# Two more k tiles by seven products in the gate/up groups of a decoder layer, with adding transfers for two of the sums

## The chip, the cores and the metric

The kernel runs on one core of one Trainium2 chip. The metric is the device time of one execution in microseconds; three executions of the kernel before gave a median of 1983.21 us.

## The reference, cut to what matters

One decoder layer on 256 tokens of width 2048, all in float32: a half-step SwiGLU feed-forward block, a token mixer, and a second half-step block, each followed by a layer norm.

```python
def _swiglu(x, w_gate, w_up, w_down):
    return (jax.nn.silu(x @ w_gate) * (x @ w_up)) @ w_down
...
    h = _layer_norm(ALPHA * h + 0.5 * _swiglu(h, ffn1_w_gate[l], ffn1_w_up[l], ffn1_w_down[l]), ...)
    mix = _mixer(h, ...)
    h = _layer_norm(ALPHA * h + mix, ...)
    h = _layer_norm(ALPHA * h + 0.5 * _swiglu(h, ffn2_w_gate[l], ffn2_w_up[l], ffn2_w_down[l]), ...)
```

`w_gate` and `w_up` are 2048x5632 each. The change is in `x @ w_gate` and `x @ w_up`, in both feed-forward blocks.

## The kernel before

Every float32 product is made of three matmuls on two reduced parts: `split` makes `hi` by a cast on ACT and `lo = src - hi` by a subtraction on DVE, and `triple` adds `xh*wh + xh*wl + xl*wh`. The moving operand is a 128x512 piece of the weights, the stationary one a 128x128 piece of the activations (16 k tiles of 128 rows by 2 blocks of 128 tokens).

The gate and up weights are laid out side by side in chunks of 512 columns, 22 chunks per feed-forward block. The first two chunks are done by `project`. The other 20 are done in ten **groups** of two chunks (`w0`, `w1`) by `Hybrid.group`. There are two such blocks in the layer, so 20 groups. A weight block read from memory is 128x1024 (two k tiles of one chunk, 512 KB) and is called j = 0 to 7.

In a group the k tiles 0 to 7 (blocks j = 0 to 3 of both chunks) are taken by **seven products** in place of eight (a scheme of Strassen's kind on two halves of k by two chunks, and two halves of k by two token blocks). The weights' quarters are "11" (`w0`, j 0 and 1), "12" (`w1`, j 0 and 1), "21" (`w0`, j 2 and 3), "22" (`w1`, j 2 and 3); each is two blocks, halves s = 0 and 1. The products are called forms 1, 5, 6, 7, 2, 4, 3. Form 5 wants 11+12, form 6 wants 11+12+22, form 7 wants 12+22, form 4 wants 11+12+22+21; forms 1, 2 and 3 take 11, 21 and 22 as they are. The sums are made in place in the tiles `sraw` by DVE (line 344). The activations' seven forms are made once per feed-forward block by `Seven`. The k tiles 8 to 15 (blocks j = 4 to 7 of each chunk) are taken plainly.

The work is a row of **units**. A unit of a form's half has 6 matmuls, a plain unit 12. Each unit has a load (SP asks for the block), a preparation (a sum where there is one, and `split` into a pair of `wring` tiles) and its matmuls. In a group the units stand in this order, with "1.0" for form 1 half 0 and "p4" for the plain block j = 4 of `w0` (a prime for `w1`): 1.0 1.1 p4, 5.0 5.1 p5, 6.0 6.1 p6, 7.0 7.1 p7, 2.0 2.1 p4', 4.0 4.1 p5', 3.0 3.1 p6' p7'. That is 14 x 6 + 8 x 12 = 180 matmuls.

What sets the order and holds the units back:

- `look(3, 4)` lets loads run up to three units ahead of their preparation and preparations up to four ahead of their matmuls.
- There are six `wring` pairs in these groups (`set_ring(6)`). The ACT cast of a unit can begin only when PE is done with the unit six before it.
- Plain blocks land in four rotating tiles `raw`, the quarters in `sraw` tiles of their own. A load waits until the last reader of its tile is done, and SP issues loads in order.
- Within these limits a scheduler orders each engine's instructions when the program is built; on the chip each engine runs its list in order.
- The bank sums of a group are finished by `sum_done`: DVE `gus` (128x512, line 728), ACT `sg`, DVE `hb` (128x256, line 719), and after every group two DVE transposes `blocks` and eight POOL transfers `hT` (line 608).
- Activations and most buffers live in 40 slots of 4 KB per partition (`act_tile`).

Of the kernel before, what the change touches and what calls it, by code (L numbers as in the profile page):

```python
# [11 lines left out]
F32 = mybir.dt.float32  # L12
# [47 lines left out]
def layer_kernel(ctx: ExitStack, tc: tile.TileContext, a: dict, out: bass.AP):  # L60
# [188 lines left out]
    class Seven:  # L249


        def __init__(self, raws, order=None, plain=None):

            self.raws, self.order, self.plain = raws, order, plain
            self.at_ = {}
            self.steps = [self.sums, lambda: self.pair(self.fa, 5, 6), lambda: self.pair(self.fb, 7, 3),
                          self.as_is, self.minus]

        def as_is(self):
# [38 lines left out]
    class Hybrid:  # L298


        def __init__(self, x, seven, k_tiles, small=False):

            self.x, self.seven, self.k_tiles = x, seven, k_tiles
            self.raws = {n: [act_tile([P, 1024], F32, "sraw") for _ in range(2)] for n in ("11", "12", "22")}
            self.raws["21"] = self.raws["12"] if small else [act_tile([P, 1024], F32, "sraw") for _ in range(2)]
            self.snaps = [[act_tile([P, 2, 512], F32, "snap") for _ in range(2)] for _ in range(1 if small else 2)]
            self.last = (3, 2, 4) if small else (2, 4, 3)
            self.turn = 0

        def group(self, w0, w1, done):  # L310
            banks = {}
# [3 lines left out]
            R = self.raws  # L315
            blocks = {"11": (w0, 0), "12": (w1, 0), "21": (w0, 2), "22": (w1, 2)}

            plan = {1: ("11", "11", None, "X"), 5: ("12", "11", ("11", "12"), "Z"), 6: ("22", "11", ("11", "22"), "X"),
# [14 lines left out]
            def seventh(p, s):  # L333
# [3 lines left out]
                def load():  # L337
                    w, j0 = blocks[load_block]
                    nc.sync.dma_start(R[load_block][s], w[j0 + s])

                def prep():
                    t = R[src][s]
                    if add is not None:
                        V.tensor_tensor(out=t, in0=t, in1=R[add[1]][s], op=ALU.add)  # L344
                    pair = next_pair()
                    split(*pair, t)
                    st["pair"] = [v.rearrange("p (g n) -> p g n", g=G) for v in pair]

                def now():
# [11 lines left out]
            def plain(n, j, last=False):  # L361
# [24 lines left out]
                unit(load, prep, now)  # L386

            end = self.k_tiles // G - 1
            for p, n, j in zip((1, 5, 6, 7) + self.last, (0, 0, 0, 0, 1, 1, 1), (4, 5, 6, 7, 4, 5, 6)):
                for s in range(2):  # L390
                    seventh(p, s)
                plain(n, j)
            plain(1, end, True)
# [311 lines left out]
    def ffn(n, x, wgu, wdn, residual, g, bt, each, first=None, between=None, nxt=None, cols=None):  # L705
# [40 lines left out]

        seven = Seven(x.raws)

# [15 lines left out]
        look(3, 4)  # L764
        hy = Hybrid(x, seven, KD)
        for p in range(1, KF // 4):
            if p == KF // 4 - 1:
                for i, q in enumerate((3, 4, 0)):
                    later(3 + 3 * i, lambda q=q: get_h(q))
                later(13, lambda: split_h(3))  # L770
                later(16, lambda: split_h(4))
            hy.group(wgu[2 * p], wgu[2 * p + 1],
                     lambda n, b, bank, snap, op, p=p: sum_done(2 * p + n, b, bank, snap, op))
        ln = LayerNorm(0.5, residual, g, bt, each, nxt, cols, ((24, 26, 48, 50), (94, 97, 100, 103)))
# [426 lines left out]

    xq = Acts(KD, "x", (0, 1))

# [117 lines left out]
```

## Time and profile before

| | |
|---|---|
| median of 3 executions | 1983.21 us (1982.7 to 1984.22) |
| the profiled execution | 1983.64 us, of which span 1981.9 us |
| matmuls | 8832 |
| PE, DVE, ACT, POOL busy | 1967.9, 1770.4, 1247.6, 248.8 us |
| groups of the first block | from about 60 to 460 us of the span |
| groups of the second block | from about 1340 to 1740 us of the span |

The span runs from the first to the last instruction; the rest of the execution's time lies around it. Engines are PE (matmuls), PEld (loads of the stationary operand), DVE, ACT, POOL and SP (which issues transfers). A busy time is the union of the durations of an engine's instructions, and on DVE and PE an instruction is issued before the one ahead of it has ended. So the time that one costs in a full queue is the distance from start to start, not its duration.

### The profile page before, as it was taken

How to read it: one execution, taken by the hardware profiler on the slowest of the kernel's cores; microseconds unless marked ns; L12 is line 12 of the kernel's file. 1: busy time of each engine (PE TensorE's matmuls, PEld its weight loads, DVE VectorE, ACT ScalarE, POOL GpSimd, SP SyncE). 2: the span in 40 equal slices, each digit the busy share in tenths (PEclk: the TensorE clock that was granted, in tenths of full speed). 3: DMA queues.
4: the chain of work that ended last, by engine and by line, in shares of the span. 5: the costliest groups of instructions: out<-in, count | busy, mean ns of one | idle time of the engine just before them, and what ended most of it. 6: DMA issues, size and time to landing. Idle time of an engine off the chain costs nothing.

```text
span 1981.9 us, 25344 instructions
## 1 busy us (share of the span) xinstructions
PE 1967.9 (99%) x8832; PEld 1628.9 (82%) x8832; DVE 1770.4 (89%) x2089; ACT 1247.6 (63%) x1571; POOL 248.8 (13%) x463
## 2 busy tenths in 40 slices
PE   9999999999999999999999999999999999999997
PEld 7888888888888888888888888888888888888886
DVE  7999999999799889999877676799999999998986
ACT  6666666666556566666667764566666666665552
POOL 0111101012010011002223130001011100121000
PEclk9999999999999999999999999999999999999999
DMA  8667766658678666677667667657676666596763
GB/s 323 220 212 237 262 211 202 218 199 313 232 228 274 204 221 246 220 245 250 228 215 249 228 225 264 220 208 242 225 257 229 201 216 228 186 327 225 256 222 125
DMA packets 133649, 460.50 MB, mean 232 GB/s; under 512 B 19424, under 2 KB 19472, under 8 KB 133520
## 3 DMA queue, kind: packets, MB, share of 16 engines
q1 hardware_dynamic: 109296, 389.59, 57.4%
q0 software_dynamic: 24224, 69.29, 11.2%
q8 instruction: 69, 1.13, 0.2%
q14 instruction: 60, 0.49, 0.1%
HBM read 429.97 MB, written 28.84 MB: 231 GB/s over the span
## 4 chain that ended last, share of the span: by engine, by line
PE 90%; DVE 4%; DMA 3%; issue 2%; ACT 1%; SPq 0%; POOL 0%; DVEq 0%; ACTq 0%; POOLq 0%
PE mm L203 29%; PE mm L204 29%; PE mm L202 29%; DVE wring L150 2%; DMA raw<-in_dn_dram 1%; PE tr L203 1%; PE tr L204 1%; PE tr L202 1%; ACT wring L149 1%; DVE sraw L344 0%; PE tr L571 0%; DMA hraw<-hT 0%; DMA raw<-in_wgd_dram 0%; DMA raw<-in_gu_dram 0%; DVE sraw L519 0%
## 5 line engine op out<-in xcount | busy, mean ns | idle before, releaser
L149 ACT CAST wring<-raw 128x1024 fp32r<-128x1024 f32 (+2 forms) x499 | 516.2, 1039 | 338.7 <-PE mm L204 236.6
L150 DVE TENSOR_TENSOR wring<-raw,wring 128x1024 fp32r<-128x1024 f32 (+2 forms) x499 | 596.7, 1202 | 117.0 <-ACT wring L149 110.3
L149 ACT CAST wring<-sraw 128x1024 fp32r<-128x1024 f32 x436 | 453.7, 1052 | 217.4 <-PE mm L204 98.1
L150 DVE TENSOR_TENSOR wring<-sraw,wring 128x1024 fp32r<-128x1024 f32 x436 | 523.6, 1217 | 35.2 <-ACT wring L149 31.0
L204 PE MATMUL mm<-wring,h 128*128 128x512 f32 (+2 forms) x1296 | 499.3, 386 | 0.0
L203 PE MATMUL mm<-wring,h 128*128 128x512 f32 (+2 forms) x1296 | 498.5, 385 | 0.3 <-DVE wring L150 0.3
L202 PE MATMUL mm<-wring,h 128*128 128x512 f32 (+2 forms) x1296 | 498.6, 385 | 0.0
L203 PE MATMUL mm<-wring,xs 128*128 128x512 f32 x776 | 302.3, 390 | 0.3 <-DVE wring L150 0.3
L202 PE MATMUL mm<-wring,xs 128*128 128x512 f32 x776 | 302.5, 390 | 0.0
L204 PE MATMUL mm<-wring,xs 128*128 128x512 f32 x776 | 302.1, 389 | 0.0
L204 PEld LDWEIGHTS mm<-wring,h 128*128 128x128 f32 x1296 | 243.5, 188 | 48.9 <-DVE h L150 1.4
L202 PEld LDWEIGHTS mm<-wring,h 128*128 128x128 f32 x1296 | 243.5, 188 | 48.8 <-ACT h L149 1.0
L203 PEld LDWEIGHTS mm<-wring,h 128*128 128x128 f32 x1296 | 243.5, 188 | 48.7 <-DVE wring L150 0.9
L344 DVE TENSOR_TENSOR sraw<-sraw,sraw 128x1024 f32<-128x1024 f32 x208 | 249.9, 1211 | 1.6 <-DMA sraw<-in_gu_dram 1.5
L608 POOL DMA_DIRECT2D hT<-blocks x176 | 95.7, 551 | 766.5 <-DVE blocks L606 711.5
L203 PEld LDWEIGHTS mm<-wring,xs 128*128 128x128 f32 x776 | 145.7, 188 | 31.5 <-DVE wring L150 1.6
L202 PEld LDWEIGHTS mm<-wring,xs 128*128 128x128 f32 x776 | 145.7, 188 | 31.1 <-ACT snap L321 0.7
L204 PEld LDWEIGHTS mm<-wring,xs 128*128 128x128 f32 x776 | 145.7, 188 | 30.1
L203 PE MATMUL mm<-wring,x 128*128 128x512 f32 x384 | 149.6, 390 | 0.6 <-DVE wring L150 0.6
L202 PE MATMUL mm<-wring,x 128*128 128x512 f32 x384 | 149.5, 390 | 0.3 <-ACT wring L149 0.3
L204 PE MATMUL mm<-wring,x 128*128 128x512 f32 x384 | 149.3, 389 | 0.0
L203 PEld LDWEIGHTS mm<-wring,x 128*128 128x128 f32 x384 | 72.1, 188 | 16.2 <-DVE wring L150 1.3
(268 smaller groups left out, 1921.2 us busy)
## 6 DMA issues: line engine op xcount, KB each, us to landing
raw<-in_gu_dram SPq DMA_DIRECT2D x191, 512.0 KB, 4.4
sraw<-in_gu_dram SPq DMA_DIRECT2D x160, 512.0 KB, 5.2
raw<-in_dn_dram SPq DMA_DIRECT2D x140, 512.0 KB, 4.6
sraw<-in_dn_dram SPq DMA_DIRECT2D x36, 512.0 KB, 5.3
hraw<-hT POOLq DMA_DIRECT2D x68, 256.0 KB, 5.7
raw<-in_w_out_dram SPq DMA_DIRECT2D x32, 512.0 KB, 4.4
raw<-in_wgd_dram SPq DMA_DIRECT2D x24, 512.0 KB, 4.6
hT<-blocks POOLq DMA_DIRECT2D x176, 64.0 KB, 2.3
```

What stands on the lines that cost most here:

```text
L149: S.copy(hi, src)
L150: V.tensor_tensor(out=lo, in0=src, in1=hi.bitcast(F32), op=ALU.subtract)
L202: PE.matmul(o, xh, wh, start=first, stop=False, skip_group_check=again)
L203: PE.matmul(o, xh, wl, start=False, stop=False, skip_group_check=again)
L204: PE.matmul(o, xl, wh, start=False, stop=last, skip_group_check=again)
L344: V.tensor_tensor(out=t, in0=t, in1=R[add[1]][s], op=ALU.add)
L608: nc.gpsimd.dma_start(to.rearrange("(g r) (i f) -> i r g f", g=4, i=4)[i], t[32 * i:32 * (i + 1), :].rearrange("r (g f) -> r g f", g=4))
```

## The change

The k tiles 8 and 9 (block j = 4 of both chunks) are taken by seven products as well: the four 128x512 quarters of it are a11, a21 (tile `u0`, from `w0`) and a12, a22 (tile `u1`, from `w1`). Two plain units of 12 matmuls become four units `n1`, `n5`, `n6`, `n7` that hold the forms (1, 2), (5, 4), (6) and (7, 3), with 6, 6, 3 and 6 matmuls. A group has 177 matmuls. Their sums are four DVE additions of 128x512. The two blocks are loaded by `load_nine` while the group before is under way, into tiles `nine` of their own. The units now stand so: 1.0 n1 1.1 p5, 5.0 n5 5.1 p6, 6.0 n6 6.1 p7, 7.0 n7 7.1, 2.0 2.1 p5', 4.0 4.1 p6', 3.0 3.1 p7'.

Of the eight 128x1024 additions on DVE four stay (forms 5 and 6). For form 7 the quarter 22 is added to 12, and for form 4 the quarter 21 to 11, by transfers from memory that add into the `sraw` tile; POOL issues them, four a group. The quarter 21 goes through the four `raw` tiles. The activations' forms of k tiles 8 and 9 are made once per block by `Seven.ninth`, which keeps a third raw quad of the activations; the forms 2 and 4 are taken from the tiles that the plain units use.

```diff
-    def __init__(self, raws, order=None, plain=None):
+    def __init__(self, raws, order=None, plain=None, ninth=False):
...
+            if ninth:
+                self.steps.insert(3, self.ninth)
...
-            self.raws["21"] = self.raws["12"] if small else [act_tile([P, 1024], F32, "sraw") for _ in range(2)]
+            self.small = small
+            if small:
+                self.raws["21"] = self.raws["12"]
+            else:
+                self.nine = [act_tile([P, 2, 512], F32, "nine") for _ in range(3)]
...
+        def load_nine(self, w0, w1):
+            for t, w in zip(self.nine, (w0, w1)):
+                nc.sync.dma_start(t.rearrange("p a n -> p (a n)"), w[4])
...
+            adds = {} if self.small else {5: ("12", "22"), 6: ("11", "21")}
...
-                    nc.sync.dma_start(R[load_block][s], w[j0 + s])
+                    if load_block == "21" and not self.small:
+                        st["raw"] = wpool.tile([P, 1024], F32, tag="raw", name=nm("raw"), bufs=4)
+                    nc.sync.dma_start(st["raw"] if "raw" in st else R[load_block][s], w[j0 + s])
 
                 def prep():
-                    t = R[src][s]
-                    if add is not None:
+                    t = st["raw"] if "raw" in st else R[src][s]
+                    if add is not None and (self.small or p in (5, 6)):
                         V.tensor_tensor(out=t, in0=t, in1=R[add[1]][s], op=ALU.add)
                     pair = next_pair()
                     split(*pair, t)
...
+                    if p in adds:
+                        to, block = adds[p]
+                        w, j0 = blocks[block]
+                        nc.gpsimd.dma_start(R[to][s], w[j0 + s], accum_op=ALU.add)
...
+            def ninth(p):
+                u0, u1, v = self.nine
+                a11, a21, a12, a22 = u0[:, 0], u0[:, 1], u1[:, 0], u1[:, 1]
+                forms = {1: (1, 2), 5: (5, 4), 6: (6,), 7: (7, 3)}[p]
+                names = {1: "XY", 5: "ZW", 6: "X", 7: "XZ"}[p]
...
+                    src = {1: u0, 5: v, 6: u0[:, 0:1], 7: u1}[p]
+                    if p == 5:
+                        for out, in0, in1 in ((v[:, 0], a11, a12), (a11, v[:, 0], a22), (v[:, 1], a11, a21)):
+                            V.tensor_tensor(out=out, in0=in0, in1=in1, op=ALU.add)
+                    elif p == 7:
+                        V.tensor_tensor(out=a12, in0=a12, in1=a22, op=ALU.add)
+                    split(*(t[:, :len(forms)] for t in pair), src)
...
+                for p, n, j in zip((1, 5, 6, 7) + self.last, (0, 0, 0, None, 1, 1, None), (5, 6, 7, None, 5, 6, None)):
+                    seventh(p, 0)
+                    if p in (1, 5, 6, 7):
+                        ninth(p)
+                    seventh(p, 1)
+                    if n is not None:
+                        plain(n, j)
+                    if p == 4 and following is not None:
+                        self.load_nine(*following)
             plain(1, end, True)
...
-        seven = Seven(x.raws)
+        seven = Seven(x.raws, None, x, True)
...
+        hy.load_nine(wgu[2], wgu[3])
...
-    xq = Acts(KD, "x", (0, 1))
+    xq = Acts(KD, "x", (0, 1, 2))
...
-    h2 = Acts(KD, "h2", (0, 1))
+    h2 = Acts(KD, "h2", (0, 1, 2))
```

The prediction speaks of three places in a group. The first is on DVE, behind the preparation of unit 7.1. Before, `sraw_82` and `sraw_83` are quarter 21, `sraw_76` and `sraw_77` quarter 11, and the rows are 2.0, the sum for 4 and its splits:

```order
L150 TENSOR_TENSOR wring_19_119<-sraw_83_457,wring_18_118 128x1024
L344 TENSOR_TENSOR sraw_76_450<-sraw_76_450,sraw_82_456 128x1024
L150 TENSOR_TENSOR wring_17_117<-raw_178_1481,wring_16_116 128x1024
L344 TENSOR_TENSOR sraw_77_451<-sraw_77_451,sraw_83_457 128x1024
L150 TENSOR_TENSOR wring_15_115<-sraw_76_450,wring_14_114 128x1024
L150 TENSOR_TENSOR wring_5_105<-sraw_77_451,wring_4_104 128x1024
```

In the changed program `sraw_77` and `sraw_78` are quarter 11, `sraw_79` and `sraw_80` quarter 12, `nine_83` is `u0`, `nine_84` is `u1`, and `nine_85` is the sums' tile. The same stretch, on DVE:

```order
L150 TENSOR_TENSOR wring_5_105<-sraw_78_457,wring_4_104 128x1024
L150 TENSOR_TENSOR wring_19_119<-nine_84_463,wring_18_118 128x1024
L150 TENSOR_TENSOR wring_17_117<-sraw_80_459,wring_16_116 128x1024
L150 TENSOR_TENSOR wring_15_115<-raw_179_1514,wring_14_114 128x1024
L150 TENSOR_TENSOR wring_5_105<-raw_180_1524,wring_4_104 128x1024
L436 TENSOR_TENSOR nine_85_464<-nine_83_462,nine_84_463 128x512
L150 TENSOR_TENSOR wring_3_103<-raw_181_1532,wring_2_102 128x1024
L438 TENSOR_TENSOR nine_84_463<-nine_84_463 128x512
L150 TENSOR_TENSOR wring_21_121<-sraw_77_456,wring_20_120 128x1024
L150 TENSOR_TENSOR wring_19_119<-sraw_78_457,wring_18_118 128x1024
```

Rows one to five are the splits of 6.1, n7, 7.1, 2.0 and 2.1. The row L436 is the next group's first sum of the ninth block: the scheduler put it three splits behind the last reader (n7) of the tile that the next group's `u1` is loaded into.

The second place is SP's list of loads over the same time. Before, with `sraw_78` quarter 12:

```order
L339 DMA sraw_78_452<-in_gu1_dram 128x1024
L368 DMA raw_184_1565<-in_gu1_dram 128x1024
L339 DMA sraw_79_453<-in_gu1_dram 128x1024
L339 DMA sraw_82_456<-in_gu1_dram 128x1024
L368 DMA raw_188_1605<-in_gu1_dram 128x1024
```

Now:

```order
L404 DMA raw_182_1565<-in_gu1_dram 128x1024
L371 DMA sraw_79_458<-in_gu1_dram 128x1024
L336 DMA nine_84_463<-in_gu1_dram 128x1024
L371 DMA sraw_80_459<-in_gu1_dram 128x1024
L404 DMA raw_183_1594<-in_gu1_dram 128x1024
```

The load of `u1` for the next group stands between the two of quarter 12.

The third place is POOL's list, which before holds only the `hT` transfers in a group:

```order
L608 DMA hT1_122<-blocks_171_1394 32x4x128 x4
L608 DMA hT1_122<-blocks_172_1400 32x4x128 x4
L736 DMA hraw_324_3111<-hT1_122 128x512 x2
L608 DMA hT1_122<-blocks_197_1692 32x4x128 x4
L608 DMA hT1_122<-blocks_198_1698 32x4x128 x4
```

Now a group has its four adding transfers (L383) around them:

```order
L383 DMA sraw_79_458<-in_gu1_dram 128x1024
L681 DMA hT1_122<-blocks_147_1113 32x4x128 x4
L681 DMA hT1_122<-blocks_148_1119 32x4x128 x4
L383 DMA sraw_80_459<-in_gu1_dram 128x1024
L383 DMA sraw_77_456<-in_gu1_dram 128x1024
L383 DMA sraw_78_457<-in_gu1_dram 128x1024
```

The one into `sraw_80` stands behind the eight `hT` transfers; the one into `sraw_78` can start when the split of 6.1 is done.

More of the change, by code (lines that the diff above doesn't have):

```diff
@@ L308, in __init__, with group @@
             self.turn = 0
-        def group(self, w0, w1, done):
+        def load_nine(self, w0, w1):
+            for t, w in zip(self.nine, (w0, w1)):
+                nc.sync.dma_start(t.rearrange("p a n -> p (a n)"), w[4])
+        def group(self, w0, w1, done, following=None):
             banks = {}
@@ L772, in ffn @@
             hy.group(wgu[2 * p], wgu[2 * p + 1],
-                     lambda n, b, bank, snap, op, p=p: sum_done(2 * p + n, b, bank, snap, op))
+                     lambda n, b, bank, snap, op, p=p: sum_done(2 * p + n, b, bank, snap, op),
+                     (wgu[2 * p + 2], wgu[2 * p + 3]) if p < KF // 4 - 1 else None)
         ln = LayerNorm(0.5, residual, g, bt, each, nxt, cols, ((24, 26, 48, 50), (94, 97, 100, 103)))
```

38 lines of the change are left out of this document (33 added, 5 removed).

## The prediction

> **What bounds the kernel now.** I read the page first, for the whole; then the windows of the gate/up groups; then the timeline of DVE, ACT and PE inside one group; and last the loads.
>
> ```profile
> span 1981.9 us, 25344 instructions
> PE 1967.9 (99%) x8832; PEld 1628.9 (82%) x8832; DVE 1770.4 (89%) x2089; ACT 1247.6 (63%) x1571; POOL 248.8 (13%) x463
> ...
> PE 90%; DVE 4%; DMA 3%; issue 2%; ACT 1%; SPq 0%; POOL 0%; DVEq 0%; ACTq 0%; POOLq 0%
> ```
>
> PE is busy all the time and carries 90% of the chain that ended last, so a matmul less should be time less. The windows show how much room the others have where the change is made (after the busy times: granted clock, share of the DMA engines, GB/s):
>
> ```profile
> 140.00:180.00 40.00, 40.00 (x179) 33.10 (x178) 38.75 (x41) 25.58 (x31) 3.53 (x7) 1.00 0.66 219
> 1420.00:1460.00 40.00, 40.00 (x178) 33.14 (x177) 38.75 (x41) 25.58 (x31) 3.54 (x7) 1.00 0.65 220
> 460.00:500.00 40.00, 40.00 (x178) 33.13 (x177) 38.16 (x49) 27.11 (x36) 13.04 (x24) 1.00 0.94 332
> ```
>
> In the groups (first two rows) PE is never idle and DVE is busy 38.75 of 40 us: two engines at their bound, PE just ahead. ACT has room.
>
> **What the groups' instructions cost.** The timeline of two groups, DVE, then ACT, then PE (start, duration):
>
> ```profile
> 207.08 0.42 DVE L719 TENSOR_TENSOR hb<-gus,sg 128x256 f32<-128x256 f32 x1
> 207.42 1.22 DVE L344 TENSOR_TENSOR sraw<-sraw,sraw 128x1024 f32<-128x1024 f32 x1
> 208.56 1.21 DVE L150 TENSOR_TENSOR wring<-sraw,wring 128x1024 fp32r<-128x1024 f32 x1
> 209.69 1.22 DVE L150 TENSOR_TENSOR wring<-raw,wring 128x1024 fp32r<-128x1024 f32 x1
> 214.23 0.68 DVE L728 TENSOR_TENSOR gus<-mm,snap 128x512 f32<-128x512 f32 x1
> 214.83 1.21 DVE L150 TENSOR_TENSOR wring<-sraw,wring 128x1024 fp32r<-128x1024 f32 x1
> 223.03 3.49 DVE L150 TENSOR_TENSOR wring<-sraw,wring 128x1024 fp32r<-128x1024 f32 x3
> 226.43 1.22 DVE L344 TENSOR_TENSOR sraw<-sraw,sraw 128x1024 f32<-128x1024 f32 x1
> ```
>
> ```profile
> 248.00 1.05 ACT L149 CAST wring<-sraw 128x1024 fp32r<-128x1024 f32 x1 [0.71 <-PE mm L204]
> ```
>
> ```profile
> 216.47 0.39 PE L202 MATMUL mm<-wring,xs 128*128 128x512 f32 x1
> 227.35 0.39 PE L202 MATMUL mm<-wring,xs 128*128 128x512 f32 x1
> 257.27 0.39 PE L202 MATMUL mm<-wring,xs 128*128 128x512 f32 x1
> ```
>
> From start to start a DVE instruction costs 1.135 us at 1024 columns (207.42 to 208.56 to 209.69), 0.60 at 512 (214.23 to 214.83) and 0.34 at 256 (207.08 to 207.42). The PE rows are unit 1.1 of one group (216.47), its unit 6.1, 48 matmuls later (227.35), and 1.1 of the next group, 180 matmuls later (257.27): 10.88/48 = 40.80/180 = 0.2267 us each. A group before takes 40.8 us.
>
> **Matmuls.** 3 fewer in each of 20 groups: 60 x 0.2267 = 13.6 us. If PE stayed busy, the time would be 1983.6 - 13.6 = 1970.0, and a group 177 x 0.2267 = 40.1 us.
>
> **DVE's work.** Before, a group has 22 splits and 8 sums of 1024, four `gus` and two transposes of 512, four `hb`: 30 x 1.135 + 6 x 0.60 + 4 x 0.34 = 39.0 us. After: 20 splits and 4 sums of 1024, in the ninth block 3 splits of 1024, one of 512 and four sums of 512, the rest the same: 27 x 1.135 + 11 x 0.60 + 4 x 0.34 = 38.6. So DVE gains 0.4 us and PE 0.7: DVE may stand still 1.5 us in a group where it could 1.8. ACT gets 1.5 casts more, in the 14 us it has free in 40. `Seven.ninth` and the dropped `as_is` split of the feed-forward forms are a few DVE instructions once per block, in the second plain chunk; there DVE prepares 8 units in the time of 96 matmuls (9 of 21.8 us), which hides them, and some 3 us would be their price without it. SP issues 16 loads a group as before, and the `raw` tiles still turn eight times (two plain blocks less, the two of quarter 21 more), so neither costs by itself.
>
> **The lead between DVE and PE.** What counts is whether each split is ready before its matmuls. Before, the split of 1.1 starts 216.47 - 208.56 = 7.9 us ahead of its matmuls. From there to the split of 6.1 (the second of the three from 223.03, at 224.16) DVE needs 15.6 us and PE 10.9, so 3.2 us are left, less the split's own 1.22: PE finds 6.1 ready by 2.0 us. After, the cast of 1.1 waits for PE's end with the unit six before it (the ACT row's wait on PE is this one). That unit is p6', and 36 matmuls lie between it and 1.1 where there were 42. So the lead at 1.1 is at most 36 x 0.2267 - 1.05 (cast) - 0.1 = 7.0 us. From 1.1 to 6.1 DVE now has 12 rows of 1024, 7 of 512 and 2 of 256: 18.5 us; PE has 57 matmuls: 12.9. Left: 7.0 - 5.6 - 1.22 = 0.2 us. PE still just fits. Any DVE wait beyond about 1.4 us a group (1.5, less a little) goes to PE in full.
>
> **The ninth block's load, the term that decides.** DVE's list has the next group's first ninth sum four rows behind the split of n7, which is the last reader of the `nine` tile to be loaded. The load goes out 1.25 us after that split starts; DVE is at the sum after 4 x 1.135 = 4.5 us. So DVE waits L - 3.3 us, L being the load's time to landing; behind it in DVE's list stand the splits of p5', 4.0 and 4.1; ACT's casts for them are not held. The loads of the groups from 100 to 420 us, 64 of line 339, and the medians of like transfers over the whole span, with POOL's at the end:
>
> ```profile
> L339 SPq DMA_DIRECT2D sraw<-in_gu_dram x64: 327/328/444, 104.1 to 405.7; - x64
> ...
> DMA to landing us min/median/max: 3.1/5.0/7.1
> ```
>
> ```profile
> raw<-in_gu_dram SPq DMA_DIRECT2D x191, 512.0 KB, 4.4
> ...
> z<-in_x_dram POOLq DMA_DIRECT2D x4, 512.0 KB, 8.4
> gb<-in_ln_b_dram POOLq DMA_DIRECT2D x6, 512.0 KB, 5.2
> ```
>
> ```profile
> L608 POOL DMA_DIRECT2D hT<-blocks x176 | 95.7, 551 | 766.5 <-DVE blocks L606 711.5
> ```
>
> L is 3.1 to 7.1; the wait 0 to 3.8 us. SP's list puts a load of quarter 12 just ahead and another just behind, and an adding transfer (into `sraw_78`, released by the split before n7's) runs beside it, so I take 5.4, nearest to the median 5.0 and somewhat above: a wait of 2.1. That is 0.7 over the 1.4, so a group takes 40.1 + 0.7 + 0.3 (ACT's `snap` copies and the 0.2 us fit at 6.1, both of which I can place no closer than this) = 41.1 us, 0.3 over before: +6 us over 20 groups.
>
> **The adding transfers.** No row shows one. From below it is a POOL load (5.2 us, the `gb` row), from above twice the slowest kind (16.8, 2 x the `z` row). Into `sraw_79` and `sraw_77` there are 16 and 10 us before the cast that reads them. Into `sraw_80` it must wait for POOL's eight `hT` issues (0.55 us each) and has 8; into `sraw_78`, from the split of 6.1 to the cast of 4.1, DVE's rows leave 6.75 us, and with the 2.1 of the ninth block's wait 8.9. At 8.4, the nearest loaded case, this hides; each us beyond costs 20 us in all. For the transfer engines:
>
> ```profile
> q1 hardware_dynamic: 109296, 389.59, 57.4%
> ```
>
> By this row 0.524 MB cost 1.53 us of all 16 engines, four more a group 6.1: the share goes from 0.66 to about 0.81. The window 460:500 above has 0.94 with PE full, so share alone doesn't stop PE; it lengthens L.
>
> [...]
>
> **The ends of the blocks.** In the last group of each block the split of an `h` tile, which lay elsewhere before, now stands ahead of the split of 6.1, where nothing is to spare:
>
> ```profile
> 236.75 1.29 DVE L150 TENSOR_TENSOR h<-hraw,h 128x512 fp32r<-128x512 f32 x2
> ```
>
> Two of 512 cost 1.2 us, twice: +2.4 us. Bounds: 0 if the lead is larger there, 6 if POOL's `hraw` issues ahead of the adding transfers make these late too.
>
> **Sum.** -13.6 (matmuls) + 20 x 1.0 (0.7 + 0.3 of waits) + 2.4 = +8.8 on the profiled execution's 1983.6 gives 1992.4; that execution lies 0.4 above the median of the three, so against the median 1992.
>
> **Rivals.** *Faster*: the ninth load lands in 4.4 us or less (the median of `raw`). Then DVE waits 1.1, inside the 1.4, and PE is fed but for the 0.3: 20 x (0.7 - 0.3) = 8 us gained, less 2.4, or all 13.6 if those small terms vanish: 1970 to 1978. For it: before, PE never waits in spite of DVE's 97%. It turns at L of about 4.7. Against it: three more transfers beside this load. *No change*: L of 4.8 to 5.1, 1979 to 1987. [...] *The change doesn't do what it says*: excluded for the matmuls, which the lists show 60 fewer.
>
> **How the numbers follow.** Slower by waits as summed 0.38 (1987 to 2010); adding transfers late 0.13 (2010 to 2060); no change 0.17; faster 0.32. About 0.2% (4 us) is what a measurement here can tell from no change. So faster 0.32, same 0.17, slower 0.51, and the time 1992. The range runs from 1969, the whole 13.6 gained, to 2025, which leaves out most of the late transfers; the slower case's own range is 1987 to 2010.
>
> **What would show it.** PE with idle time before unit 5.1 or 6.1, released by DVE's split; DVE idle at the sum of line 436, released by the DMA of `nine`, about 2 us in each group; groups 41 us apart; no wait of ACT on `sraw` beyond a few tenths. Wrong if the sum of line 436 waits under 1.2 us (then faster), or if ACT's casts of `sraw` wait on POOL's transfers (then slower by more).

## The result, and the profile after

The changed kernel takes 2047.18 us (median of 6 executions, 2044.87 to 2052.33) against 1983.20 us (6 executions, 1982.7 to 1984.22): ratio 1.0325, 95% interval 1.0311 to 1.0338. It is 64 us slower, and 55 us slower than predicted. The profiled execution took 2048.91 us. Its page:

```profile
span 2046.8 us, 25513 instructions
...
PE 1984.4 (97%) x8772; PEld 1629.2 (80%) x8772; DVE 1759.0 (86%) x2139; ACT 1269.3 (62%) x1613; POOL 319.9 (16%) x543
...
PE 58%; DVE 25%; DMA 8%; issue 6%; ACT 1%; POOL 0%; SPq 0%; DVEq 0%; ACTq 0%; POOLq 0%
```

The 60 matmuls are gone (8772), yet PE is busy 17 us longer, and it carries only 58% of the chain that ended last; DVE has 25% and transfers 8%. The windows of two stretches in the groups (columns as before: PE, PEld, DVE, ACT, POOL, granted clock, share of the DMA engines, GB/s):

```profile
140.00:180.00 40.00, 37.58 (x158) 30.37 (x157) 35.33 (x37) 26.40 (x30) 7.91 (x12) 0.96 0.85 254
1440.00:1480.00 40.00, 37.53 (x158) 30.42 (x157) 35.34 (x39) 24.33 (x30) 7.93 (x12) 0.96 0.86 249
```

158 matmuls in 40 us where there were 179. Both engines that were full now stand still at times, and the granted clock is 0.96 where it was 1.00. From the first `gus` of a group to the next group's it is 43.9 us on average over the 18 distances inside the blocks (39.8 to 45.6, the shortest at the ends of the blocks), where it was 40.7. Twenty times the difference is 63 us, so nearly all of the loss lies in the groups. The waits (engine, line, what it waited for: us in all, times, longest):

```profile
DVE nine L436 <- DMA nine<-in_gu_dram: 78.8, 18, 6.8
...
PEld mm L203 <- DVE wring L150: 51.3, 32, 2.6
PE mm L203 <- DVE wring L150: 39.9, 29, 2.1
...
ACT wring L149 <- DMA sraw<-in_gu_dram: 31.1, 20, 3.8
```

DVE waits 18 times at the first sum of the ninth block, 4.4 us on average, and PE then waits for DVE's splits. One such wait on DVE, and SP's list before it:

```profile
197.10 1.22 DVE L150 TENSOR_TENSOR wring<-nine,wring 128x1024 fp32r<-128x1024 f32 x1
...
199.37 2.36 DVE L150 TENSOR_TENSOR wring<-raw,wring 128x1024 fp32r<-128x1024 f32 x2
208.55 0.69 DVE L436 TENSOR_TENSOR nine<-nine,nine 128x512 f32<-128x512 f32 x1 [6.82 <-DMA nine<-in_gu_dram]
```

```profile
196.08 0.33 SPq L371 DMA_DIRECT2D sraw<-in_gu_dram  x1
198.35 0.33 SPq L336 DMA_DIRECT2D nine<-in_gu_dram  x1
```

The split of n7 starts at 197.10, SP asks for `u1` at 198.35 (1.25 us later, as foreseen), and the sum starts at 208.55: this load took 10.2 us. What the transfers cost, by the DMA queues (packets, MB, share of the 16 engines' span; the first line is POOL's queue before, the rest is after) and the issues (median us to landing):

```profile
q0 software_dynamic: 24224, 69.29, 11.2%
```

```profile
q0 software_dynamic: 35744, 111.23, 22.3%
...
raw<-in_gu_dram SPq DMA_DIRECT2D x191, 512.0 KB, 5.6
...
sraw<-in_gu_dram POOLq DMA_DIRECT2D x80, 512.0 KB, 7.3
nine<-in_gu_dram SPq DMA_DIRECT2D x40, 512.0 KB, 6.8
```

POOL's queue had 11.2% of 1981.9 us before, 222 us; now 22.3% of 2046.8, 456. The 80 adding transfers so took 2.93 us of all 16 engines each.

**The clock.** The prediction did not have this. Eleven stretches of 3.41 or 6.83 us inside the groups run at half clock, 13 times 3.41 us in all; before, there was none but the one at the very end. One of them, as three windows of 3.41 us, and PE's matmuls through it:

```profile
145.00:148.41 3.41, 1.58 (x6) 1.09 (x7) 3.41 (x4) 2.40 (x3) 1.62 (x3) 0.99 0.90 236
148.41:151.82 3.41, 3.41 (x10) 2.64 (x9) 3.41 (x4) 2.48 (x3) 0.85 (x1) 0.51 1.01 203
151.82:155.23 3.41, 3.41 (x17) 2.80 (x16) 2.75 (x3) 1.81 (x2) 0.85 (x1) 1.00 1.01 217
```

```profile
147.26 0.50 PE L203 MATMUL mm<-wring,xs 128*128 128x512 f32 x1 [1.83 <-DVE wring L150]
147.59 0.39 PE L204 MATMUL mm<-wring,xs 128*128 128x512 f32 x1
...
149.08 0.63 PE L203 MATMUL mm<-wring,x 128*128 128x512 f32 x1
149.50 0.63 PE L204 MATMUL mm<-wring,x 128*128 128x512 f32 x1
149.93 0.63 PE L202 MATMUL mm<-wring,x 128*128 128x512 f32 x1
```

PE waits 1.83 us for DVE's split, is busy only 1.58 of 3.41 us, and in the next 3.41 us its matmuls come 0.427 us apart (149.08, 149.50, 149.93) in place of 0.227. Such a window holds eight matmuls, which cost 1.6 us more. If PE is the bound in all 13 windows, they cost 21 us; that is an estimate.

### The profile page after: what moved, and what is told of

Its sections match the earlier page's. It is cut to its first block, busy times and chain, and to the rows that moved or that the text cites. A ratio compares the mean times of both kernels' runs of the same rounds, so it can differ in the third digit from the quotient of the medians.

```text
span 2046.8 us, 25513 instructions
## 1 busy us (share of the span) xinstructions
PE 1984.4 (97%) x8772; PEld 1629.2 (80%) x8772; DVE 1759.0 (86%) x2139; ACT 1269.3 (62%) x1613; POOL 319.9 (16%) x543
## 3 DMA queue, kind: packets, MB, share of 16 engines
q0 software_dynamic: 35744, 111.23, 22.3%
## 4 chain that ended last, share of the span: by engine, by line
PE 58%; DVE 25%; DMA 8%; issue 6%; ACT 1%; POOL 0%; SPq 0%; DVEq 0%; ACTq 0%; POOLq 0%
PE mm L203 18%; PE mm L204 18%; PE mm L202 18%; DVE wring L150 15%; DMA nine<-in_gu_dram 6%; DVE sraw L376 3%; DVE gus L801 2%; DVE hb L792 1%; DMA sraw<-in_gu_dram 1%; DVE nine L436 1%; DVE blocks L679 1%; ACT wring L149 1%; PE tr L202 1%; PE tr L204 1%; PE tr L203 1%
## 5 line engine op out<-in xcount | busy, mean ns | idle before, releaser
L149 ACT CAST wring<-sraw 128x1024 fp32r<-128x1024 f32 x396 | 412.8, 1053 | 188.1 <-DVE sraw L376 73.6
L203 PE MATMUL mm<-wring,h 128*128 128x512 f32 (+2 forms) x1316 | 509.3, 387 | 1.4 <-DVE wring L150 1.4
L204 PE MATMUL mm<-wring,h 128*128 128x512 f32 (+2 forms) x1316 | 509.6, 387 | 0.9 <-DVE h L150 0.9
L202 PE MATMUL mm<-wring,h 128*128 128x512 f32 (+2 forms) x1316 | 509.4, 387 | 0.1
L150 DVE TENSOR_TENSOR wring<-sraw,wring 128x1024 fp32r<-128x1024 f32 x396 | 478.2, 1221 | 19.2 <-ACT wring L149 16.9
L203 PE MATMUL mm<-wring,xs 128*128 128x512 f32 x696 | 276.6, 397 | 32.9 <-DVE wring L150 32.9
L203 PEld LDWEIGHTS mm<-wring,h 128*128 128x128 f32 x1316 | 249.1, 189 | 53.0 <-DVE wring L150 3.3
L204 PEld LDWEIGHTS mm<-wring,h 128*128 128x128 f32 x1316 | 248.7, 189 | 51.6 <-DVE h L150 2.3
L202 PEld LDWEIGHTS mm<-wring,h 128*128 128x128 f32 x1316 | 249.5, 190 | 50.6 <-ACT h L149 1.1
L202 PE MATMUL mm<-wring,xs 128*128 128x512 f32 x696 | 274.6, 395 | 6.6 <-ACT wring L149 6.6
L204 PE MATMUL mm<-wring,xs 128*128 128x512 f32 x696 | 275.1, 395 | 0.0
L203 PEld LDWEIGHTS mm<-wring,xs 128*128 128x128 f32 x696 | 132.0, 190 | 66.4 <-DVE wring L150 39.5
L203 PE MATMUL mm<-wring,x 128*128 128x512 f32 x404 | 160.4, 397 | 5.6 <-DVE wring L150 5.6
L383 POOL DMA_DIRECT2D sraw<-in_gu_dram x80 | 70.6, 883 | 607.9 <-DVE sraw L376 432.2
L202 PEld LDWEIGHTS mm<-wring,xs 128*128 128x128 f32 x696 | 131.5, 189 | 39.4 <-ACT wring L149 12.6
L202 PE MATMUL mm<-wring,x 128*128 128x512 f32 x404 | 159.7, 396 | 0.0
L204 PE MATMUL mm<-wring,x 128*128 128x512 f32 x404 | 159.1, 394 | 0.0
L376 DVE TENSOR_TENSOR sraw<-sraw,sraw 128x1024 f32<-128x1024 f32 x128 | 155.5, 1219 | 2.2 <-DMA sraw<-in_wgm_dram 2.0
L204 PEld LDWEIGHTS mm<-wring,xs 128*128 128x128 f32 x696 | 132.6, 191 | 26.9
L788 ACT ACTIVATE sg<-gus 128x256 f32<-128x256 f32 x80 | 33.6, 420 | 163.3 <-DVE gus L801 163.1
```

The costliest lines, as they stand in the source:

```text
L149: S.copy(hi, src)
L150: V.tensor_tensor(out=lo, in0=src, in1=hi.bitcast(F32), op=ALU.subtract)
L202: PE.matmul(o, xh, wh, start=first, stop=False, skip_group_check=again)
L203: PE.matmul(o, xh, wl, start=False, stop=False, skip_group_check=again)
L204: PE.matmul(o, xl, wh, start=False, stop=last, skip_group_check=again)
L383: nc.gpsimd.dma_start(R[to][s], w[j0 + s], accum_op=ALU.add)
```

## The experiments

Two theories stood at the start. A: the load of `u1` is late at DVE's first ninth sum. B: the adding transfers are dear, in the transfer engines' time or at ACT's casts. All times stand beside runs of the kernel before on the same chip (1982.8 to 1983.7).

**`u1` twice.** An earlier load, with all four adding transfers kept.

```diff
-SLOTS = 40
+SLOTS = 41
...
-                self.nine = [act_tile(...) for _ in range(3)]
+                self.u0, self.v = (act_tile(...) for _ in range(2))
+                self.u1 = [act_tile(...) for _ in range(2)]
...
-                    if p == 4 and following is not None:
-                        self.load_nine(*following)
+                    if following is not None and p in (5, 4):
+                        self.load_nine(p == 5, following[p == 5])
```

> The changed kernel with two tiles for u1 (41 slots), and the load of u1 asked at form 5 of the group before, so that it is out nearly a whole group ahead of the first ninth sum. Theory A (the late load of u1 is the cause: DVE waits 78.8 us in 18 of the 20 groups for it, 3.9 a group, and the clock dips follow PE's waits): that wait is gone, groups fall from 43.9 to 40.1 to 40.8 us, the time to 1970 to 1985, the granted clock back to 0.998. Theory B (the adding transfers are the cause, by crowding the transfer engines and by arriving late at ACT's casts): the wait moves to ACT's casts of sraw, groups of 42 us or more, 2010 to 2040.

Measured: 2003.21 us, ratio 1.0102 (1.0086 to 1.0117), a group 41.9 us, four half-clock windows. DVE's wait for `nine` is gone, and ACT's wait is what is left:

```profile
ACT wring L149 <- DMA sraw<-in_gu_dram: 59.6, 37, 3.8
```

43.4 of these us are 19 waits for the fourth adding transfer, into `sraw_78`, whose median to landing is 8.6 us; the first and third are never waited for, the second 2.5 us in all, and the other 13.7 us are waits for SP's own loads. So A is 44 us, and something of B stays.

**Plain transfers** and **no transfers.** In the first POOL's four transfers are loads without the addition, in the second there are none; both leave out the additions for forms 7 and 4.

```diff
-                        nc.gpsimd.dma_start(R[to][s], w[j0 + s], accum_op=ALU.add)
+                        nc.gpsimd.dma_start(R[to][s], w[j0 + s])
```

```diff
-            adds = {} if self.small else {5: ("12", "22"), 6: ("11", "21")}
+            adds = {}
```

> The changed kernel with the four adding transfers of a group made plain loads of the same blocks to the same tiles from the same queue (the additions for forms 7 and 4 are left out). If an adding transfer costs two reads (2.92 us of the 16 engines each by the queue's share, against 1.53 for a load), share in the groups falls from 0.85 to about 0.75, the load of u1 lands in 5.5 instead of 6.8, DVE waits 2.2 for it: groups of 41 to 42 us, 1990 to 2010. If the doubled engine time plays no part, it stays above 2035.

> The changed kernel without the four transfers of a group (the additions for forms 7 and 4 are left out altogether), the rest and DVE's list as it is. Theory A with the load's place in the lists alone to blame: u1 still goes out behind n7 and lands in about 5, DVE waits 1.7 to 2, groups of 40.5 to 41.2, 1975 to 1995. Theory B: without the transfers all is well, under 1978.

Measured: 1999.86 us, 1.008 (1.0065 to 1.0095), a group 41.5 us; and 1974.47 us, 0.995 (0.9935 to 0.9964), a group 40.2 us. The wait at the ninth sum, plain and then none:

```profile
DVE nine L436 <- DMA nine<-in_gu_dram: 45.3, 17, 4.0
```

```profile
DVE nine L436 <- DMA nine<-in_gu_dram: 20.8, 18, 2.0
```

The addition alone is 47 us, four plain loads 25 more. Without them 20.8 us of DVE's waits reach the end time by almost nothing. In the plain kernel POOL's queue has 17.2% of 1998.9 us: 1.52 us of the engines for a plain load, against 2.93 with the addition.

**Transfers without the ninth block**, in the kernel before: forms 7 and 4 by adding transfers, plain units for k tiles 8 and 9 as they were.

```diff
+            small = R["21"] is R["12"]
+            adds = {} if small else {5: ("12", "22"), 6: ("11", "21")}
...
-                    if add is not None:
+                    if add is not None and (small or p in (5, 6)):
...
+                    if p in adds:
+                        to, block = adds[p]
+                        w, j0 = blocks[block]
+                        nc.gpsimd.dma_start(R[to][s], w[j0 + s], accum_op=ALU.add)
```

> The kernel before with the sums for forms 7 and 4 by adding transfers, and no ninth block. DVE has 4.5 us less to do in a group (34.5 of 40.8). Theory A: nothing waits, within 0.2% of before, 1979 to 1987. Theory B: the transfers land in about 7 and crowd the loads, ACT waits for them or for loads, PE waits: 1995 or more.

Measured: 1990.37 us, 1.0033 (1.0022 to 1.0044), between the ranges of the two theories. The windows and the waits:

```profile
140.00:180.00 40.00, 40.00 (x178) 33.14 (x177) 34.64 (x37) 25.52 (x31) 7.11 (x12) 1.00 0.91 272
```

```profile
ACT wring L149 <- DMA sraw<-in_gu_dram: 54.3, 31, 4.7
```

Here the same transfers, at a share of 0.91, cost 7 us in all. DVE has 5 us of room in 40, and PE stays full through 54 us of ACT's waits. This suggests that the late transfers become dear where DVE has no slack; no run takes DVE's slack alone away.

**All eight sums on DVE, no transfers.** Quarter 21 is held in its `raw` tiles for form 4.

```diff
-            adds = {} if self.small else {5: ("12", "22"), 6: ("11", "21")}
+            adds = {}
+            held = {}
...
-                    if add is not None and (self.small or p in (5, 6)):
-                        V.tensor_tensor(out=t, in0=t, in1=R[add[1]][s], op=ALU.add)
+                    if "raw" in st:
+                        held[s] = t
+                    if add is not None:
+                        V.tensor_tensor(out=t, in0=t, in1=held[s] if add[1] == "21" and not self.small
+                                        else R[add[1]][s], op=ALU.add)
```

> The changed kernel with all eight sums of the other blocks on DVE again and no adding transfer; the ninth block stays. Theory 'the sums had to leave DVE' (DVE is the second bound): a group costs DVE 38.6 + 4 x 1.135 = 43.1 us against PE's 40.1, so a group takes 43.1 to 43.5 and the time is 1974.5 (the kernel without the transfers and without these sums) + 20 x (43.1 - 40.2) = 2032, range 2025 to 2040; the wait for the ninth block (1.0 us a group without transfers) vanishes because DVE comes late. Rival 'DVE has room, the transfers were never needed': under 1990. DVE's wait at the sum of the ninth block: under 0.5 us a group by the first.

Measured: 2042.64 us, 1.0302 (1.0284 to 1.0319), 3 us above the range, with eight half-clock windows that were not expected; DVE has no wait for `nine`. A group takes 44.3 us on average, a little over the 43.1 that DVE's list was reckoned at, and DVE is all but full:

```profile
140.00:180.00 40.00, 36.96 (x156) 29.61 (x155) 39.05 (x41) 23.55 (x27) 4.33 (x8) 0.96 0.67 213
```

Some sums must leave DVE for the ninth block to be worth anything.

**POOL's own sums** in place of the transfers, with `u1` once and twice (the second has the edit of `u1` twice as well).

```diff
-            adds = {} if self.small else {5: ("12", "22"), 6: ("11", "21")}
+            adds = {} if self.small else {6: "12", 2: "11"}
...
-                    if p in adds:
-                        to, block = adds[p]
-                        w, j0 = blocks[block]
-                        nc.gpsimd.dma_start(R[to][s], w[j0 + s], accum_op=ALU.add)
+                    if p in adds:
+                        to = R[adds[p]][s]
+                        nc.gpsimd.tensor_tensor(out=to, in0=to, in1=R["22"][s] if p == 6 else st["raw"], op=ALU.add)
```

> The changed kernel with the sums for forms 7 and 4 made by POOL (one 128x1024 sum each, four a group, from tiles that are in SBUF already) in place of the adding transfers; nothing else moves. Theory 'the time went to the transfers and what they crowd': back to the kernel without transfers, 1974.5, plus what POOL's sums cost DVE: 1973 to 1985, the ninth block's load lands in 4.3 us and DVE waits 1.0 us a group for it. Rival 'POOL's sums are as late as the transfers, or slow DVE down while they run': no row shows a POOL sum; at 6 us or more each the cast of form 7 or 4 waits, and the group takes 42 us or more: 2005 or more. The granted clock stays at 1.00 in the groups by the first, since PE hardly waits.

> As the kernel with POOL's sums, and u1 (the second tile of the ninth block) kept twice and asked 18 matmuls and more earlier. Both suspected causes are gone: if they are all there is, PE is the bound, a group takes 177 x 0.2267 = 40.1 us and the time is 1966 to 1974, faster than both kernels. If the single u1 costs nothing once the transfers are gone, the same time as the kernel with POOL's sums alone, within 3 us. If POOL's sums slow DVE: 1990 or more.

Measured: 2130.73 us, 1.0748 (1.0732 to 1.0764), and 2129.28 us, 1.0737 (1.072 to 1.0755): the slowest of all, and the rival that POOL's sums slow DVE down holds. The wait at the ninth sum is gone in both but for one of 1.0 us, so its load plays no part. They also have 31 and 34 half-clock windows; what these add no run parts. POOL's sums and DVE's rows beside them, in one group of the first:

```profile
157.80 2.35 POOL L382 TENSOR_TENSOR sraw<-sraw,sraw 128x1024 f32<-128x1024 f32 x1
164.19 3.31 POOL L382 TENSOR_TENSOR sraw<-sraw,raw 128x1024 f32<-128x1024 f32 x1 [4.04 <-DVE wring L150]
```

```profile
155.92 1.22 DVE L150 TENSOR_TENSOR wring<-raw,wring 128x1024 fp32r<-128x1024 f32 x1
157.05 4.19 DVE L376 TENSOR_TENSOR sraw<-sraw,sraw 128x1024 f32<-128x1024 f32 x1
...
165.18 3.42 DVE L150 TENSOR_TENSOR wring<-raw,wring 128x1024 fp32r<-128x1024 f32 x1
```

Beside these two POOL sums a DVE row of 1.22 us takes 4.19 and 3.42 us, and ends 1.1 us after the sum each time; a row from 164.04 to 165.25, which overlaps the second sum as well, takes 1.21. So in these rows a POOL addition costs DVE 3.0 and 2.2 us, more than the 1.135 of an addition of its own.

**`u1` twice with plain transfers** (the additions for forms 7 and 4 left out): both edits from above together.

> u1 kept twice, and POOL's four transfers a group as plain loads without the addition (so the additions for forms 7 and 4 are left out). Against the kernel with u1 twice and adding transfers (2003) this isolates the addition where the ninth block's wait is gone; against plain transfers with one u1 (2000) it isolates the load of u1. Theory 'the late ninth block is what plain transfers cost': 1970 to 1980. Rival 'the transfers are late at ACT's casts themselves': POOL's plain loads land in 4.7 us, inside the 6.75 us there are, so ACT's waits on them would have to be over 1 us a group and the time over 1985.

Measured: 1973.60 us, 0.9952 (0.9938 to 0.9967), a group 40.2 us, no half-clock window. With this run the two causes stand in a table (us):

| | `u1` once | `u1` twice |
|---|---|---|
| adding transfers | 2047.2 | 2003.2 |
| plain transfers | 1999.9 | 1973.6 |

Either mended alone brings 44 to 47 us, the second 26 to 30 more. They overlap: the load of `u1` is also slower with the adding transfers (8.3 us against 6.1 with plain ones), and in the changed kernel 27.3 of the 28.0 us in which ACT waits for the fourth transfer lie inside DVE's waits for `u1`.

**Three transfers.** The fourth is replaced by a DVE sum at unit 2.1, where the block of quarter 21 lies in a `raw` tile anyway. With `u1` twice, and with `u1` once as in the changed kernel:

```diff
+                    if (p, s) == (2, 1) and not self.small:
+                        V.tensor_tensor(out=R["11"][1], in0=R["11"][1], in1=t, op=ALU.add)
-                    if p in adds:
+                    if p in adds and (p, s) != (6, 1):
```

> u1 kept twice; of the four adding transfers of a group the last one (into R11's second tile, behind the split of 6.1) is gone, and DVE makes that sum behind the split of 2.1, where the block is in a raw tile anyway. All of the output is computed. Theory 'one transfer of four is late and the late u1 is the other half': with both gone the waits vanish, DVE needs 38.6 + 1.1 = 39.7 us a group and PE 40.1, so a group takes 40.2 to 40.6 and the time is 1973 to 1982, faster than before. Rival 'the transfers' engine time crowds every load': the casts of sraw and raw still wait over 20 us in all and the time stays over 1990. Rival 'DVE is at its bound again': DVE 39.7 without room, PE waits over 0.5 us a group for its splits, 1982 to 1990. No half-clock stretch in the groups by the first.

> The changed kernel with u1 once, as it was; only the last adding transfer of a group is replaced by DVE's sum behind the split of 2.1. That transfer starts within 5 us of the two loads of the ninth block. If the late u1 costs its share by itself, as with plain transfers: DVE waits 1.5 to 2.5 us a group at the ninth block's sum, a group takes 41 to 41.8, 1992 to 2008. If the last transfer was what made u1 late: the load lands in about 4.5 us, and the time is 1975 to 1985.

Measured: 1975.86 us, 0.9964 (0.9951 to 0.9976), and 1973.61 us, 0.9949 (0.9935 to 0.9963). Both compute everything and beat both kernels; the second differs from the changed kernel by three lines, takes no memory, and gains 74 us on it and 10 on the kernel before. The first came out as its first theory had it. For the second neither expectation had the reason, and the time lies 1.4 us below the nearer range. `u1` still takes 6.0 us (median), but DVE comes later:

```profile
192.25 1.22 DVE L381 TENSOR_TENSOR sraw<-sraw,raw 128x1024 f32<-128x1024 f32 x1
193.38 1.22 DVE L150 TENSOR_TENSOR wring<-raw,wring 128x1024 fp32r<-128x1024 f32 x1
194.52 2.46 DVE L150 TENSOR_TENSOR wring<-sraw,wring 128x1024 fp32r<-128x1024 f32 x2
196.90 0.69 DVE L438 TENSOR_TENSOR nine<-nine,nine 128x512 f32<-128x512 f32 x1
```

The scheduler put the ninth sum behind four more rows, 9.2 us behind n7's split (4.5 us of rows in the changed kernel), and it waits for nothing. The edit thus changed two things, a transfer and the place of a sum. The next runs part them.

**The sums behind n1.** The ninth sums for forms 5 and 4 are made in place in `u0`. The reader of `u0` is n1's split, so they can't be hoisted ahead of it. All four transfers stay.

```diff
-                    src = {1: u0, 5: v, 6: u0[:, 0:1], 7: u1}[p]
+                    src = {1: u0, 5: u0, 6: v[:, 0:1], 7: u1}[p]
...
-                        for out, in0, in1 in ((v[:, 0], a11, a12), (a11, v[:, 0], a22), (v[:, 1], a11, a21)):
+                        for out, in0, in1 in ((a11, a11, a12), (v[:, 0], a11, a22), (a21, v[:, 0], a21)):
```

> The changed kernel with the ninth block's sums for forms 5 and 4 made in place in u0 (11+12 over a11, form 4 over a21, form 6 in the third tile) and everything else as it was, the four adding transfers and the single u1 too. In place, the first sum can't stand ahead of n1's split, the reader of u0: in DVE's list it moves some 12 rows back, to 8 us or more behind where it was, and u1's load (8.3 us from its issue) has 17 us. Theory 'the place of the sum in DVE's list makes u1 late, not the load': DVE's wait for nine is gone (under 5 us in all), what stays is the last adding transfer at ACT's cast (50 us in all), as with u1 twice: 1998 to 2008. Rival 'the ninth block's lateness alone is the loss': 1973 to 1985. Rival 'the sums now crowd the lead between 1.1 and 6.1': PE waits at 5.1 or 6.1, over 2010.

Measured: 2000.08 us, 1.0082 (1.0063 to 1.0102), no half-clock window in the groups, no wait for `nine`. Moving the sums is worth 47 us, as much as a second tile. What is left is the transfers, at ACT:

```profile
ACT wring L149 <- DMA sraw<-in_gu_dram: 67.9, 35, 3.4
```

**Is it the late reader or the load on the engines?** Three runs. In the first each adding transfer became two plain loads, the second into a tile that nobody reads (the additions for forms 7 and 4 left out). In the second and third the kernel with three transfers makes the fourth again, into an unread tile; the third ties it to its old place by a 4-column sum from the tile of 6.1.

```diff
-                        nc.gpsimd.dma_start(R[to][s], w[j0 + s], accum_op=ALU.add)
+                        nc.gpsimd.dma_start(R[to][s], w[j0 + s])
+                        nc.gpsimd.dma_start(self.spill, w[j0 + s])
```

```diff
...
+                    if (p, s) == (6, 1) and not self.small:
+                        V.tensor_tensor(out=self.spill[:, 0:4], in0=t[:, 0:4], in1=t[:, 0:4], op=ALU.add)
-                    if p in adds and (p, s) != (6, 1):
+                    if p in adds:
...
-                        nc.gpsimd.dma_start(R[to][s], w[j0 + s], accum_op=ALU.add)
+                        nc.gpsimd.dma_start(self.spill if (p, s) == (6, 1) else R[to][s], w[j0 + s], accum_op=ALU.add)
```

> The changed kernel with each adding transfer replaced by two plain loads of the same block by POOL, one into the tile and one behind it into a tile that nobody reads (so the additions for forms 7 and 4 are left out). Twice 1.5 us of the transfer engines against 2.9 us for an adding transfer, without an addition. If the engine time is what the adding transfers cost: as the changed kernel, a share of 0.95, the ninth block lands in 6 to 7 us, 2030 to 2050. If it is the addition's own time in a transfer that makes it late: as with single plain transfers, 2000 to 2010.

> As the kernel with three adding transfers and one u1 (1973.6), but the fourth adding transfer is still made, into a tile that nobody reads, at the same place in POOL's list. The transfer engines do all the work of the changed kernel, share about 0.95; DVE's list is that of the 1973.6 kernel. Theory 'the late readers are the loss (the ninth sum early in DVE's list, the cast of 4.1), not the engines' load': 1973 to 1982. Rival 'the engines' load by itself delays loads enough': u1 lands in about 8 us as in the changed kernel, SP's sraw loads in 7.5 us, and DVE or ACT waits over 1 us a group: 1990 to 2010.

> The last kernel with an unread fourth adding transfer had those transfers bunched at the start of the blocks, so it did not load the engines where it was meant to. Here a DVE sum of 4 columns (one a group) from the tile of 6.1 into the unread tile holds each fourth transfer back to its old place, behind the split of 6.1. Otherwise as the kernel with three transfers (1973.6); DVE's list has the ninth sum late. Theory 'late readers, not the engines' load': all groups 40.2 to 40.6, 1973 to 1982, although the transfer engines do all the work of the changed kernel. Rival 'the load of the engines counts': DMA share 0.9 or more in the groups, SP's sraw loads at 7 us or more to landing, ACT or DVE waiting over 1 us a group for loads of SP, 1990 to 2010.

Measured: 2112.20 us, 1.0633 (1.0611 to 1.0655); 2035.02 us, 1.0261 (1.0245 to 1.0278); 2007.19 us, 1.0112 (1.0092 to 1.0132). The first two lie outside every range that was expected, the third in that of its rival. The first two tell nothing: without a reader the unread transfers were moved to the start of the blocks, where each waits for the one ahead (338.3 us in 68 waits in the first run, 106.9 us in 15 in the second) and holds up POOL's queue (first groups of 47 to 58 us, later ones 39 to 43). The third loads the engines in the right place. SP's loads in the kernel with three transfers, then in the third run:

```profile
sraw<-in_gu_dram SPq DMA_DIRECT2D x120, 512.0 KB, 5.9
...
nine<-in_gu_dram SPq DMA_DIRECT2D x40, 512.0 KB, 6.2
```

```profile
sraw<-in_gu_dram SPq DMA_DIRECT2D x120, 512.0 KB, 7.8
sraw<-in_gu_dram POOLq DMA_DIRECT2D x60, 512.0 KB, 6.4
nine<-in_gu_dram SPq DMA_DIRECT2D x40, 512.0 KB, 7.5
```

An adding transfer that nobody waits for, behind the split of 6.1, takes SP's `sraw` and `nine` loads from 5.9 and 6.2 us to 7.8 and 7.5, and the time is 34 us longer. Not all of the 34 us is the load's: in the first block DVE's order differs much (the ninth sum stands 13 to 25 us behind n7's split, where the kernel with three transfers has 7 to 10), and a group takes 42.9 us against 40.4. In the second block the sum stands 9.2 us behind it in nearly all groups, as in the kernel with three transfers. There a group takes 41.2 us against 40.4, and DVE waits for `nine` again, 12.2 us in all. So the theory of the late reader alone falls: the load on the engines at that place counts by itself, some 0.8 us a group where the orders are nearly alike.

## Why the prediction was wrong, and where it was right

**Right: what PE and DVE need.** The matmul term and the lead held. Without transfers the time was 1974.5, against the 1970.0 of the matmul term, 1972.4 with the ends of the blocks (which no run parted from the rest), and the groups 40.2 us against 40.1. The prediction let DVE wait 1.4 us a group for free. That kernel waits 1.2 us 18 times, and PE loses almost nothing.

**Right: the mechanism that decides.** DVE waits at line 436, released by the DMA of `nine`, and PE waits for DVE's splits. The rule "DVE waits L - 3.3" holds at three loads, to 0.6 us. With L the median of `u1`'s load alone, its issue paired with its landing in each group, and the median wait beside it:

| kernel | L, us | L - 3.3 | wait, us |
|---|---|---|---|
| no transfers | 4.5 | 1.2 | 1.1 |
| plain transfers | 6.1 | 2.8 | 2.8 |
| changed kernel | 8.3 | 5.0 | 4.4 |

In the changed kernel DVE came to the sum 0.7 us later in 9 of the 18 groups, which is most of what the last row is short.

**The step that failed: L taken as 5.4.** It was 8.3, beyond the range of 3.1 to 7.1 that the rows of before gave. Those rows show loads at a share of 0.66; this load has its neighbours from SP and an adding transfer beside it.

**The cause of that: the adding transfers.** Without them L is 4.5, with plain loads in their place 6.1, with the addition 8.3. The prediction put 1.53 us of the engines for one, a plain load's; it is 2.93, 1.9 times a plain one's 1.52. Whether it makes two reads, as the expectation of the plain transfers supposes, is in no view here. That the addition acts through this engine time is the likeliest reading and is not shown: the run with two plain loads, which was to part the two, bunched its loads elsewhere.

**"At 8.4 this hides" failed for one transfer of four.** The bounds of 5.2 and 16.8 held the landing of nearly all (5.1 to 9.9 us, median 7.3). Three of four are hidden, but for 1.4 us in all. The one into `sraw_78` lands 8.6 us (median) after its issue, and ACT waits 28.0 us for it in 15 groups. The prediction had put 8.9 us of room there. One group, POOL's issue and ACT's casts of 4.0 and 4.1:

```profile
197.49 0.86 POOL L383 DMA_DIRECT2D sraw<-in_gu_dram  x1 [3.11 <-DVE wring L150]
```

```profile
202.67 1.06 ACT L149 CAST wring<-sraw 128x1024 fp32r<-128x1024 f32 x1 [0.30 <-PE mm L204]
207.50 1.05 ACT L149 CAST wring<-sraw 128x1024 fp32r<-128x1024 f32 x1 [3.77 <-DMA sraw<-in_gu_dram]
```

The split of 6.1 starts at 195.97, POOL issues 1.5 us later, and ACT is ready for 4.1 at 203.73, 7.8 us after the split's start (7.7 to 9.3 in the groups that wait). The 8.9 counted DVE's wait of 2.1 as room, though ACT's casts are not held by it, as the prediction says itself. In the changed kernel this can have cost little by itself, since DVE stood still at the same time (27.3 of the 28.0 us); with DVE's wait gone it is what is left. The case of late transfers, 0.13 for 2010 to 2060, would have been nearer than 1992, though DVE's wait and not this one made up the loss. No run shows the term that this range was reckoned from; in the changed kernel these transfers land after 7.3 us (median) and 9.9 at most.

**Missing: the clock.** No term had it. The sum with the measured sizes comes out: the missed 55 us are 2.8 us a group. DVE's 78.8 us over 20 groups are 3.9 a group where 2.1 were put, 1.8 more; the half-clock windows are 21/20, 1.0. ACT's waits are not in it, as they lie inside DVE's. That this sum fits is bookkeeping: the runs part the load of `u1` from the addition, but none takes the clock alone away. From the other end: 1973.6 + 18 x (4.4 - 1.4) + 21 = 2049, against 2047.

**What stays open.** Why `u1` and its neighbours land late when the engines' share is 0.85 to 0.91 and not 1 was not tried further. In the kernel with three transfers the place of the ninth sum and the missing fourth transfer both help, and the tied run, whose order on DVE differs in the first block, parts them only in part.

## What to carry to other kernels

Where two engines are within 3% of each other, price a new wait by what the later load will take beside the new transfers, not by loads in today's traffic: here a load went from a median of 5.0 to 8.3 us, and by the estimate above each microsecond beyond 1.4 came out of every group. Look first for the place of the waiting instruction in its engine's list; moving it behind other work brought as much as a second buffer. Moving work from a full engine to transfers pays piece by piece: three of the four transfers were hidden, and giving the fourth back to the full engine, which also moved the ninth sum, made the difference between 64 us lost and 10 gained.

## What the runs showed of the hardware that was not expected

- **An adding transfer** of 512 KB costs 2.93 us of the 16 transfer engines against 1.52 plain. In the same kernel with plain and with adding transfers, POOL's landed after 4.7 and 7.3 us (medians).
- **Half clock came behind windows with idle PE.** In the changed kernel the half-clock stretches, but for the one at the end of the run, are 3.41 or 6.83 us long and stand on a fixed grid of 3.41 us. Beyond the first 40 us, no full-clock window of that grid with under 1.72 us of idle PE was followed by a half-clock one; of the seven with 1.72 to 1.89 six were, and all six with 2.15 or more. It mattered how a wait fell on the grid: the wait of 1.83 us that ended at 147.26 lay inside one window and was followed by half clock; a wait of 2.13 us that left 1.50 us idle in one window and 0.63 in the next was not.
- **DVE rows grew beside POOL's sums.** Beside two POOL sums of 2.35 and 3.31 us, DVE rows of 1.22 us became 4.19 and 3.42 us.
